# Where seven products and their weight sums stand among the up steps of an MLP

## The chip, the core and the metric

One core of a Trainium2 chip runs the whole program. The metric is device time in microseconds (us), lower is better. Of the engines, five names matter here: PE (TensorE, matmuls), DVE (VectorE), ACT (ScalarE), POOL (GpSimd, which here only issues DMAs) and SP (SyncE, which issues the other DMAs). Each engine runs its instructions in the order in which the compiled program lists them.

## The reference

Two residual layers of width D = 2048 over 256 tokens, in fp32: a convolution module, an MLP, a state-space layer, a second MLP, a final norm. The change touches the second MLP alone:

```python
def mlp(h, w_up, w_down):
    a = jax.nn.relu(h @ w_up)          # w_up 2048 x 8192
    return (a * a) @ w_down            # w_down 8192 x 2048
...
    h = rms_norm(x, mlp_norm[i])
    x = x + mlp(h, mlp_w_up[i], mlp_w_down[i])
return rms_norm(x, final_norm)
```

## The kernel before

**Precision.** Each fp32 weight block is split in two fp32r parts: ACT copies it to `hi` (L148) and DVE forms `lo = block - hi` (L155). Products are taken with both parts. A block is one *step* of the program, loaded, split and multiplied in two *halves* of 128 x 1024 elements (`run_steps`, L194). The four `hi` and four `lo` buffers let the split run up to four halves ahead of the products (L207); loads are issued four steps ahead (L205), and the six `raw` buffers hold three steps.

**The second MLP** works in eight slices s of 1024 hidden features.

- `up(s, k)`, written u0 to u7 below: eight steps that form slice s of `h @ w_up`. A half is 16 matmuls, eight with `hi` (L236, 512 columns) and eight with `lo` (L239, 256 columns). Every second one (odd k) ends with `relu2_forms` (L960), on ACT and DVE, which squares the activations and writes eight linear forms of them to `rT`.
- `seven(s, n)`, L753: the product with `w_down` for 1024 output columns, by a scheme of the Strassen-Winograd kind: seven products of 2 x 2 blocks where eight would be usual. They need sums of weight blocks. Its eight steps are called a0 to a7 for the first columns (n = 0) and b0 to b7 for the second (n = 2). A half of a product step is six matmuls of 512 columns (L743 to L745). The steps are:
  - a0: load block B01 into Y (POOL; no product).
  - a1: load B00, product A11; on DVE, X = B00 + Y, one add for each half.
  - a2: product S1 with X, nothing loaded.
  - a3: load B11, product S4; on DVE, X = B11 + X.
  - a4: product S2 with X, nothing loaded.
  - a5: a DMA of POOL adds B11 onto Y in place (L123), product S3 with Y.
  - a6: load B10, product A12.
  - a7: a DMA of POOL adds B10 onto X in place, product A22 with X.
  The sums of a1 and a3 are the adds at L161. Each product is taken into `x` by DVE (L772).

**Order.** A table in `mlp` (L905 to L909) lists the steps of round s: the eight up steps of slice s + 1 among the products of slice s. Rounds 0 to 5 have the same table; rounds 6 and the end have others. A scheduler at compile time then places instructions on each engine by readiness and priority; the split and the sums have a higher priority (`high_priority`, L147). `behind(ins)` (L451) holds it to one thing: what is issued inside comes after `ins`. Blocks for u, a1, a3 and a6 are loaded by SP in step order; those for a0, a5 and a7 by POOL.

Of the kernel before, what the change touches and what calls it, by code (L numbers as in the profile page):

```python
# [14 lines left out]
ALU = mybir.AluOpType  # L15
# [22 lines left out]
class Trunk:  # L38
# [97 lines left out]
    def split(self, h, urgent=True):  # L136
        i, half = divmod(h, 2)
        _, chain, consume, pre = self.steps[i]
        if consume is None:
            return None  # L140
        if pre == "x":
            sl = chain[half]
        else:
            sl = self.raws.pop(h)
        hi = self.w.tile(list(sl.shape), F32R, tag="hi", name="hi", bufs=4)
        lo = self.w.tile(list(sl.shape), F32R, tag="lo", name="lo", bufs=4)
        with self.tc.high_priority(offset=URGENT if urgent else 0):  # L147
            self.nc.scalar.activation(hi, sl, AF.Copy)  # L148
            eng = self.nc.gpsimd if i in self.pool_lo else self.nc.vector
            if self.barrier is not None and h == 2 * self.barrier + 2:  # L150
                self.low_late = lambda: eng.tensor_tensor(out=lo, in0=sl, in1=hi.bitcast(F32), op=ALU.subtract)
                self.parts[h] = (hi, lo)
                return None
            with self.behind(self.lo_gate) if self.lo_gate is not None else nullcontext():
                ins = eng.tensor_tensor(out=lo, in0=sl, in1=hi.bitcast(F32), op=ALU.subtract)  # L155
            self.lo_gate = None
            if i in self.also:
                to, first = self.also[i]
                if first is not None:
                    to[half] = self.wide.tile(list(sl.shape), F32, tag="wd", name="sum")  # L160
                self.tt(to[half], sl, (to if first is None else first)[half], ALU.add)  # L161
            if i in self.pool_lo:
                self.pool_ins = ins
            else:
                self.lo_ins = ins
        self.parts[h] = (hi, lo)
        return ins
# [566 lines left out]
    def mlp(self, layer, last_slice, last_block, hooks=None):  # L734
# [60 lines left out]
        def up(s, only=None):  # L795
            for q in range(4):
                for kc in range(2):
                    if only is not None and only != 2 * q + kc:
                        continue

                    def consume(hi, lo, half, q=q, kc=kc):
                        if kc == 0 and half == 0:
                            if formed(s):
                                if q % 2 == 0:
                                    rT.setdefault(s, []).append(self.blk_tile([P, 2, 2, 8, P], F32R, name="rT"))
                            elif q == 0:
                                rT[s] = self.blk_tile([P, 8, 2, T], F32R, name="rT")
                            rT["uacc"] = self.acc2()
                        A = rT["uacc"]
                        self.mm_f([A[:, 0], A[:, 1]], self.hT, hi, lo, kc * 8 + half * 4,  # L810
                                  kc == 0 and half == 0, kc == 1 and half == 1)
                        if kc == 1 and half == 1:
                            if s == 0 and q == 1 and layer == 0:
                                self.rate = 2.75
                            if formed(s):
                                act = lambda: self.relu2_forms(A, rT[s][q // 2][:, q % 2])
                            else:
                                act = lambda: self.relu2(A, rT[s], 2 * q)
                            act()
                    self.add_f(w_up, kc * 8, s * 1024 + q * 256, consume)  # L820
# [75 lines left out]
        m = [[seven(s, n) for n in (0, 2)] for s in range(nsl)]  # L896
        for k in range(7):
            up(0, k)
        m[0][0][0]()
        up(0, 7)  # L900
        for s in range(nsl - 1):
            u = [partial(up, s + 1, k) for k in range(8)]
            a, b = m[s]
            if s < nsl - 2:
                order = (u[0], a[1], a[2], u[1], a[3], a[4], u[2], a[5], a[6], u[3], b[0], a[7], b[1], u[4], b[2], b[6],  # L905
                         u[5], b[3], b[4], u[6], b[5], u[7], m[s + 1][0][0], b[7])
            else:
                order = (u[0], a[1], u[1], a[2], u[2], a[3], u[3], a[4], u[4], u[5], a[5], u[6], a[6], u[7],
                         m[s + 1][0][0], a[7])  # L909
            for e in order:  # L910
                e()
        a = m[-1][0]
# [854 lines left out]
```

## Time and profile before

| | |
|---|---|
| median of 3 runs | 1958.6 us (1958.26 to 1959.34) |
| profiled execution | 1959.17 us, span 1957.0 us |
| busy in the span | PE 99%, DVE 81%, ACT 55%, POOL 19% |
| rounds 0 to 5 of the second MLP | 1313.8 to 1819.6 us of the span |
| mean granted TensorE clock | 0.998 |

In a row of the timeline the first number is the start in us from the start of the span, the second the duration; an idle time before it and what ended that stand in brackets. Consecutive matmuls overlap in the records: the time that one takes of PE is the distance to the next one's start. The same holds on DVE, with a smaller overlap.

### The profile page before, as it was taken

To read this page: it belongs to the slowest core of one execution; us is meant where nothing else is said; L and a number is where in the kernel's file an instruction comes from. 1 tells how busy PE (TensorE), PEld (TensorE's weight loads), DVE (VectorE), ACT (ScalarE), POOL (GpSimd) and SP (SyncE) were. 2 spreads that over 40 slices of the span, in tenths; PEclk is the share of its full clock that TensorE was granted. 3 is DMA by queue.
4 is the path that set the end of the run, shared out by engine and by line. 5 is a ranking of instruction groups with operands and counts; after the bars stand their busy time and mean duration, and the time that the engine had idled before them with its cause. 6 is when DMAs were issued, how large, how long until landed. Compare 5 with 4: busy or idle time off the path is not lost.

```text
span 1957.0 us, 30302 instructions
## 1 busy us (share of the span) xinstructions
PE 1931.6 (99%) x11432; PEld 1653.2 (84%) x11432; DVE 1575.4 (81%) x2148; ACT 1083.5 (55%) x1357; POOL 363.2 (19%) x334
## 2 busy tenths in 40 slices
PE   8999999999999999999999999999999999999998
PEld 8999788888888888888888788888888888888887
DVE  6899898788787676767557856578999999999986
ACT  6444655544454545454545445466666666666664
POOL 4899300000010212221101000001111111111110
PEclk9999999999999999999999999999999999999999
DMA  9668468777686878877898966677889889898984
GB/s 249 183 178 222 127 193 258 216 232 235 208 268 183 210 215 262 270 246 230 279 328 304 352 210 186 191 226 216 245 248 255 258 239 256 234 253 242 254 262 137
DMA packets 334514, 457.96 MB, mean 234 GB/s; under 512 B 16481, under 2 KB 218273, under 8 KB 331009
## 3 DMA queue, kind: packets, MB, share of 16 engines
q1 hardware_dynamic: 299184, 369.93, 59.1%
q0 software_dynamic: 31616, 81.53, 17.6%
q10 hardware_dynamic: 3568, 4.56, 0.8%
q8 instruction: 89, 1.46, 0.3%
q14 instruction: 57, 0.47, 0.1%
HBM read 429.44 MB, written 34.91 MB: 237 GB/s over the span
## 4 chain that ended last, share of the span: by engine, by line
PE 89%; DVE 5%; DMA 3%; issue 2%; ACT 1%; POOL 0%; SPq 0%; DVEq 0%; POOLq 0%; ACTq 0%
PE acc L236 22%; PE acc L239 11%; PE acc L259 10%; PE acc L260 10%; PE acc L261 10%; PE acc L248 3%; PE acc L250 3%; PE acc L249 3%; DVE lo L155 3%; DMA raw<-in_mlp_w_down_dram 2%; PE mp L744 2%; PE mp L745 2%; PE mp L743 2%; PE mr L743 1%; PE mr L744 1%
## 5 line engine op out<-in xcount | busy, mean ns | idle before, releaser
L148 ACT ACTIVATE hi<-raw 128x1024 fp32r<-128x1024 f32 x644 | 681.3, 1059 | 743.1 <-PE acc L261 305.6
L155 DVE TENSOR_TENSOR lo<-raw,hi 128x1024 fp32r<-128x1024 f32 x583 | 708.1, 1221 | 275.7 <-ACT hi L148 274.4
L236 PE MATMUL acc<-hT,hi 128*128 128x512 f32 x2048 | 515.5, 393 | 0.0
L236 PEld LDWEIGHTS acc<-hT,hi 128*128 128x128 f32 x2048 | 372.4, 189 | 70.5 <-issue 1.6
L239 PEld LDWEIGHTS acc<-hT,lo 128*128 128x128 f32 x2048 | 279.3, 190 | 20.3 <-DVE lo L155 0.3
L239 PE MATMUL acc<-hT,lo 128*128 128x256 f32 x2048 | 286.1, 282 | 0.0
L259 PE MATMUL acc<-hi,rT 128*128 128x512 f32 x496 | 194.2, 392 | 0.0
L260 PE MATMUL acc<-lo,rT 128*128 128x512 f32 x496 | 193.4, 390 | 0.0
L261 PE MATMUL acc<-hi,rT 128*128 128x512 f32 x496 | 193.0, 389 | 0.0
L123 POOL DMA_DIRECT2D sum<-in_mlp_w_down_dram x56 | 68.1, 1231 | 462.5 <-DVE lo L155 301.0
L155 POOL TENSOR_TENSOR lo<-raw,hi 128x1024 fp32r<-128x1024 f32 x60 | 144.1, 2416 | 30.1 <-ACT hi L148 22.9
L248 PE MATMUL acc<-hT,hi 128*128 128x256 f32 x512 | 146.0, 286 | 1.0 <-ACT hi L148 1.0
L249 PE MATMUL acc<-hT,hi 128*128 128x256 f32 x512 | 145.2, 285 | 0.0
L250 PE MATMUL acc<-hT,lo 128*128 128x256 f32 x512 | 144.7, 285 | 0.1
L988 DVE SCALAR_TENSOR_TENSOR cv<-vT,dw,cv 128x256 f32<-128x256 f32 x348 | 140.9, 482 | 2.6 <-ACT cv L575 2.2
L148 ACT ACTIVATE hi<-sum 128x1024 fp32r<-128x1024 f32 x112 | 118.6, 1059 | 43.1 <-PE acc L236 26.2
L155 DVE TENSOR_TENSOR lo<-sum,hi 128x1024 fp32r<-128x1024 f32 x112 | 135.9, 1218 | 7.7 <-ACT hi L148 7.4
L259 PEld LDWEIGHTS acc<-hi,rT 128*128 128x128 f32 x496 | 93.1, 188 | 20.8 <-issue 1.6
L261 PEld LDWEIGHTS acc<-hi,rT 128*128 128x128 f32 x496 | 93.1, 188 | 19.4
L260 PEld LDWEIGHTS acc<-lo,rT 128*128 128x128 f32 x496 | 93.1, 188 | 19.0 <-issue 0.2
L248 PEld LDWEIGHTS acc<-hT,hi 128*128 128x128 f32 x512 | 98.5, 192 | 3.7 <-issue 2.1
L259 PE MATMUL acc<-hi,yT 128*128 128x512 f32 x256 | 101.1, 395 | 0.0
(324 smaller groups left out, 2957.9 us busy)
## 6 DMA issues: line engine op xcount, KB each, us to landing
raw<-in_mlp_w_up_dram SPq DMA_DIRECT2D x256, 512.0 KB, 4.8
raw<-in_mlp_w_down_dram SPq DMA_DIRECT2D x228, 512.0 KB, 5.5
sum<-in_mlp_w_down_dram POOLq DMA_DIRECT2D x84, 512.0 KB, 7.9
raw<-in_conv_w_in_dram SPq DMA_DIRECT2D x128, 256.0 KB, 3.9
raw<-in_ssm_w_glu_dram SPq DMA_DIRECT2D x64, 512.0 KB, 4.1
raw<-in_conv_w_out_dram SPq DMA_DIRECT2D x32, 512.0 KB, 4.2
Vd<-bv POOLq DMA_DIRECT2D x16, 512.0 KB, 5.3
Md<-Kd POOLq DMA_DIRECT2D x32, 256.0 KB, 6.9
```

The lines of the kernel that those rows point to most:

```text
L123: self.nc.gpsimd.dma_start(out=chain[hf], in_=view[:, k], accum_op=ALU.add)
L148: self.nc.scalar.activation(hi, sl, AF.Copy)
L155: ins = eng.tensor_tensor(out=lo, in0=sl, in1=hi.bitcast(F32), op=ALU.subtract)
L236: mm(accs[m], lhsT=hi[:, kk, cs[m]], rhs=xT(k0 + kk), start=first and kk == 0, stop=False)
L239: mm(accs[m][:, 0:T], lhsT=lo[:, kk, cs[m]], rhs=xT(k0 + kk)[:, 0, :], start=False, stop=last and kk == 3)
L248: mm(accs[m], lhsT=hi[:, kk, c], rhs=x[:, 0, :], start=first and kk == 0, stop=False)
L249: mm(accs[m], lhsT=hi[:, kk, c], rhs=x[:, 1, :], start=False, stop=False)
L250: mm(accs[m], lhsT=lo[:, kk, c], rhs=x[:, 0, :], start=False, stop=last and kk == 3)
L259: mm(acc[:, b, :], lhsT=ak[:, 0, t], rhs=hi[:, kk, :], start=first and kk == 0, stop=False)
L260: mm(acc[:, b, :], lhsT=ak[:, 0, t], rhs=lo[:, kk, :], start=False, stop=False)
L261: self.mm_last = mm(acc[:, b, :], lhsT=ak[:, 1, t], rhs=hi[:, kk, :], start=False, stop=last and kk == 1)
L988: return self.nc.vector.scalar_tensor_tensor(out=out, in0=a, scalar=s, in1=b, op0=op0, op1=op1)
```

## The change

Two things. In `split`, the add for X at L161 is issued `behind(ins)`, where `ins` is the subtraction that forms `lo` of the same half. And the tables of rounds 0 to 6 are written anew: the product steps stand one at a time or in twos between up steps, and b7 and a0 of the next slice move from the end of a round to behind the first up step of the next round (`late`).

```diff
                     to[half] = self.wide.tile(list(sl.shape), F32, tag="wd", name="sum")
-                self.tt(to[half], sl, (to if first is None else first)[half], ALU.add)
+                with self.behind(ins):
+                    self.tt(to[half], sl, (to if first is None else first)[half], ALU.add)
...
+        late = []
         for s in range(nsl - 1):
             u = [partial(up, s + 1, k) for k in range(8)]
             a, b = m[s]
             if s < nsl - 2:
-                order = (u[0], a[1], a[2], u[1], a[3], a[4], u[2], a[5], a[6], u[3], b[0], a[7], b[1], u[4], b[2], b[6],
-                         u[5], b[3], b[4], u[6], b[5], u[7], m[s + 1][0][0], b[7])
+                order = [u[0], *late, a[1], u[1], a[2], u[2], a[3], a[4], u[3], a[5], a[6], u[4], a[7], b[0], b[1],
+                         u[5], b[2], b[6], u[6], b[3], b[4], u[7], b[5]]
+                late = [b[7], m[s + 1][0][0]]
             else:
-                order = (u[0], a[1], u[1], a[2], u[2], a[3], u[3], a[4], u[4], u[5], a[5], u[6], a[6], u[7],
-                         m[s + 1][0][0], a[7])
+                order = [u[0], *late, a[1], u[1], a[2], u[2], a[3], u[3], a[4], u[4], u[5], a[5], u[6], a[6], u[7],
+                         m[s + 1][0][0], a[7]]
```

The instructions of the engines are the same in kind and number; their places differ. In the rows below the number behind a name tells buffers of one name apart; it differs between the two programs.

DVE in round 1, about step b3, before. `sum_13733` and `sum_13739` are X of the b steps, `raw_13830` and `raw_13832` the block of b3, `raw_13758` and `raw_13760` that of b6, `raw_13784` and `raw_13786` that of u5:

```order
L155 TENSOR_TENSOR lo_13811<-raw_13758,hi_13810 128x1024
L979 TENSOR_TENSOR sum_13733<-raw_13830,sum_13733 128x1024
L979 TENSOR_TENSOR sum_13739<-raw_13832,sum_13739 128x1024
L988 SCALAR_TENSOR_TENSOR v_13709<-v_13709,u_13708 128x128
L155 TENSOR_TENSOR lo_13835<-raw_13760,hi_13834 128x1024
L155 TENSOR_TENSOR lo_13846<-raw_13784,hi_13845 128x1024
L988 SCALAR_TENSOR_TENSOR x_83<-mr_13838,r2_12254,x_83 128x512
L155 TENSOR_TENSOR lo_13857<-raw_13786,hi_13856 128x1024
L274 TENSOR_TENSOR rT_13383<-v_13709,rT_13383 128x512
L155 TENSOR_TENSOR lo_13868<-raw_13830,hi_13867 128x1024
```

The same place after. `raw_13888` and `raw_13890` are the block of b3, `sum_13785` and `sum_13798` are X, `raw_13804` and `raw_13806` the block of b6, `raw_13830` and `raw_13832` that of u6:

```order
L155 TENSOR_TENSOR lo_13855<-raw_13804,hi_13854 128x1024
L155 TENSOR_TENSOR lo_13893<-raw_13806,hi_13892 128x1024
L970 TENSOR_TENSOR t_13874<-acc_13738,t_13874 128x512
L155 TENSOR_TENSOR lo_13904<-raw_13830,hi_13903 128x1024
L991 SCALAR_TENSOR_TENSOR x_83<-mr_13896,r2_12254,x_83 128x512
L155 TENSOR_TENSOR lo_13915<-raw_13832,hi_13914 128x1024
L155 TENSOR_TENSOR lo_13926<-raw_13888,hi_13925 128x1024
L982 TENSOR_TENSOR sum_13785<-raw_13888,sum_13785 128x1024
L982 TENSOR_TENSOR v_13876<-u_13875 128x2x128
L991 SCALAR_TENSOR_TENSOR x_83<-mq_13918,r2_12254,x_83 128x512
L155 TENSOR_TENSOR lo_13942<-raw_13890,hi_13941 128x1024
L982 TENSOR_TENSOR sum_13798<-raw_13890,sum_13798 128x1024
```

Before, both sums on b3's block stand ahead of the second `lo` of b6 and of both of u5, and eight rows ahead of the first `lo` of their own block. After, each stands right behind the `lo` of its own half, and every `lo` of the steps before b3 is ahead of it.

DVE in round 1, about steps a3 and a4, before. `rT_13026` is the second half of the forms of this round's slice (u6 and u7 of the round before), which S1 (a2) reads; `raw_13421` and `raw_13423` are the block of a3, `raw_13373` and `raw_13375` that of u1:

```order
L979 TENSOR_TENSOR sum_13364<-raw_13421,sum_13364 128x1024
L274 TENSOR_TENSOR rT_13026<-u_13325,rT_13026 128x512
L988 SCALAR_TENSOR_TENSOR v_13326<-v_13326,u_13325 128x128
L979 TENSOR_TENSOR sum_13381<-raw_13423,sum_13381 128x1024
L155 TENSOR_TENSOR lo_13437<-raw_13373,hi_13436 128x1024
L988 SCALAR_TENSOR_TENSOR v_13326<-v_13326,u_13325 128x128
L155 TENSOR_TENSOR lo_13448<-raw_13375,hi_13447 128x1024
L988 SCALAR_TENSOR_TENSOR x_83<-mp_13429,r2_12254,x_83 128x512
L155 TENSOR_TENSOR lo_13459<-raw_13421,hi_13458 128x1024
L155 TENSOR_TENSOR lo_13475<-raw_13423,hi_13474 128x1024
L274 TENSOR_TENSOR rT_13026<-v_13326,rT_13026 128x512
L155 TENSOR_TENSOR lo_13496<-sum_13364,hi_13495 128x1024
```

The same place after. `rT_12971` is that second half of the forms, `raw_13388` and `raw_13390` the block of u1, `sum_13402` and `sum_13415` X (whose `lo` is that of a2), `raw_13421` and `raw_13423` the block of u2, `raw_13447` the first half of that of a3:

```order
L155 TENSOR_TENSOR lo_13418<-raw_13388,hi_13417 128x1024
L991 SCALAR_TENSOR_TENSOR x_83<-mp_13046,r2_12254,x_83 128x512
L155 TENSOR_TENSOR lo_13426<-raw_13390,hi_13425 128x1024
L155 TENSOR_TENSOR lo_13437<-sum_13402,hi_13436 128x1024
L275 TENSOR_TENSOR rT_12971<-v_13309,rT_12971 128x512
L991 SCALAR_TENSOR_TENSOR x_83<-mp_13429,r2_12254,x_83 128x512
L155 TENSOR_TENSOR lo_13452<-sum_13415,hi_13451 128x1024
L155 TENSOR_TENSOR lo_13472<-raw_13421,hi_13471 128x1024
L155 TENSOR_TENSOR lo_13506<-raw_13423,hi_13505 128x1024
L970 TENSOR_TENSOR t_13491<-acc_13355,t_13491 128x512
L155 TENSOR_TENSOR lo_13517<-raw_13447,hi_13516 128x1024
L982 TENSOR_TENSOR sum_13402<-raw_13447,sum_13402 128x1024
```

Before, the last row of `relu2_forms` (`rT_13026<-v_13326`) stands behind the sums of a3, the four `lo` of u1 and a3 and behind both `lo` of a2, which are ahead of these rows; after, it stands between the two `lo` of a2, with u1 ahead of it and u2 and a3 behind it.

SP, the loads from the end of one round into the next; a row of `x2` is one block, since each half is one DMA:

```order
 L102 DMA raw<-in_mlp_w_up_dram 128x4x256 x2
 L102 DMA raw<-in_mlp_w_down_dram 128x2x512 x2
-L102 DMA raw<-in_mlp_w_up_dram 128x4x256 x6
+L102 DMA raw<-in_mlp_w_up_dram 128x4x256 x4
+L102 DMA raw<-in_mlp_w_down_dram 128x2x512 x2
+L102 DMA raw<-in_mlp_w_up_dram 128x4x256 x4
 L102 DMA raw<-in_mlp_w_down_dram 128x2x512 x2
 L102 DMA raw<-in_mlp_w_up_dram 128x4x256 x2
```

Where three blocks of `w_up` in a row (u6, u7 and u0 of the next round) came before, there are now at most two. POOL's DMAs stand in the same order as before.

## The prediction

> **What bounds the kernel now.** The page first:
>
> ```profile
> PE 1931.6 (99%) x11432; PEld 1653.2 (84%) x11432; DVE 1575.4 (81%) x2148; ACT 1083.5 (55%) x1357; POOL 363.2 (19%) x334
> ```
>
> PE is the bound, and the change takes no work from it. What can be won is time in which PE waits in rounds 0 to 5 of the second MLP, so the busy time by stage is read next, one stretch for each round (columns: stretch, length, then busy time of PE, PEld, DVE, ACT and POOL, granted clock, DMA share, GB/s):
>
> ```profile
> 1399.10:1481.80 82.70, 81.91 (x419) 69.35 (x418) 76.70 (x89) 55.39 (x63) 12.56 (x13) 1.00 0.91 250
> sum 505.80, PE 498.77 PEld 423.21 DVE 468.96 ACT 336.24 POOL 74.20; mean PE 83.13 PEld 70.53 DVE 78.16 ACT 56.04 POOL 12.37
> ```
>
> Three things lie close together: in 505.8 us PE's records leave 7.0 us open, DVE is busy 78.2 us of 84.3 in a mean round, and the DMA engines are about 0.9 busy. To know what PE loses, I need the price of its work where nothing waits, from PE's timeline:
>
> ```profile
> 1330.93 0.39 PE L744 MATMUL mr<-lo,rT 128*128 128x512 f32 x1
> ...
> 1335.69 0.39 PE L745 MATMUL mp<-hi,rT 128*128 128x512 f32 x1
> 1335.91 1.98 PE L236 MATMUL acc<-hT,hi 128*128 128x512 f32 x8
> 1337.73 1.12 PE L239 MATMUL acc<-hT,lo 128*128 128x256 f32 x8
> 1338.68 0.63 PE L236 MATMUL acc<-hT,hi 128*128 128x512 f32 x2
> ```
>
> Between 1330.93 and 1335.91 start 22 product matmuls: 0.2264 us each. A half of an up step takes 1338.68 - 1335.91 = 2.77 us. So an up step is 5.54 us, a product step (12 matmuls) 2.72 us, and a round (8 up steps, 14 product steps) 44.32 + 38.04 = 82.4 us. Six rounds are 494.2 us against 505.8: **PE loses 11.6 us**, 0.6% of the time, and no change of order can win more here. It is more than the 7.0 us of open time because a matmul that waited overlaps nothing, and because of one slow stretch, below. The waits of PE over these rounds (total, times, longest):
>
> ```profile
> PE mp L744 <- DVE lo L155: 3.1, 5, 0.6
> PE mq L744 <- DVE lo L155: 2.9, 3, 1.9
> PE mr L745 <- DVE rT L274: 1.0, 3, 0.6
> ```
>
> All end in DVE, and they are of two families. `mq` is product A12 (b6), `mp` and `mr` are those of a2 to a4.
>
> **Family B: a sum that waits for a DMA, with others behind it.** Timelines of DVE, PE and SP in round 0, and a stretch about it in the form of the table above:
>
> ```profile
> 1362.01 0.28 DVE L988 SCALAR_TENSOR_TENSOR v<-v,u 128x128 f32<-128x128 f32 x1
> 1366.17 1.23 DVE L979 TENSOR_TENSOR sum<-raw,sum 128x1024 f32<-128x1024 f32 x1 [3.88 <-DMA raw<-in_mlp_w_down_dram]
> 1367.31 1.22 DVE L155 TENSOR_TENSOR lo<-raw,hi 128x1024 fp32r<-128x1024 f32 x1
> 1368.45 1.22 DVE L979 TENSOR_TENSOR sum<-raw,sum 128x1024 f32<-128x1024 f32 x1
> ```
>
> ```profile
> 1366.28 0.39 PE L745 MATMUL mr<-hi,rT 128*128 128x512 f32 x1
> 1368.59 0.50 PE L744 MATMUL mq<-lo,rT 128*128 128x512 f32 x1 [1.93 <-DVE lo L155]
> 1370.30 3.36 PE L236 MATMUL acc<-hT,hi 128*128 128x512 f32 x8
> 1373.50 0.40 PE L744 MATMUL mq<-lo,rT 128*128 128x512 f32 x1
> ```
>
> ```profile
> 1356.46 2.16 SPq L102 DMA_DIRECT2D raw<-in_mlp_w_down_dram  x2
> ```
>
> ```profile
> 1360.00:1380.00 20.00, 18.07 (x87) 15.00 (x86) 15.84 (x18) 9.61 (x11) 1.10 (x1) 0.91 0.77 234
> ```
>
> SP issued b3's block at 1356.46 and it landed about 9.7 us later. DVE stood before b3's sum for 3.9 us, though the `lo` of b6 that PE needed at 1366.5 was next in its queue. PE started 2.08 us late (2.31 from start to start, less 0.23). Then eight L236 took 3.20 us instead of 1.82, another 1.4; with 0.3 about it the one event cost 3.8 us. The other two waits of `mq` (2.9 - 1.9 = 1.0 us) cost about 1.5 with the same 0.3 about each. Family B: 5.3 us.
>
> The slow stretch behind the wait shows in the granted clock: 0.91 in the last row, the 20 us about it. The Trainium skill, "TensorE: Matmul & The Clock Gate", Part 1 (the HAM clock gate), says that the clock halves after an idle window of about 3.4 us. By that rule a wait of 2.1 us would cost itself alone, and family B would be 1.4 us less; the row shows that it did cost them, so here rule and row differ.
>
> **Family A: too much of DVE's work in a row.** The five waits of `mp` in the list are one in each of rounds 1 to 5, among a2 to a4, some with one of `mr` ahead. Round 1, PE and DVE:
>
> ```profile
> 1416.84 0.39 PE L743 MATMUL mp<-hi,rT 128*128 128x512 f32 x1
> 1417.39 0.50 PE L745 MATMUL mr<-hi,rT 128*128 128x512 f32 x1 [0.16 <-DVE rT L274]
> 1418.53 0.50 PE L744 MATMUL mp<-lo,rT 128*128 128x512 f32 x1 [0.63 <-DVE lo L155]
> ```
>
> ```profile
> 1416.65 0.69 DVE L274 TENSOR_TENSOR rT<-v,rT 128x512 fp32r<-128x512 f32 x1
> 1417.26 1.22 DVE L155 TENSOR_TENSOR lo<-sum,hi 128x1024 fp32r<-128x1024 f32 x1
> 1418.39 0.68 DVE L967 TENSOR_TENSOR t<-acc,t 128x512 f32<-128x512 f32 x1
> 1418.99 0.74 DVE L988 SCALAR_TENSOR_TENSOR x<-mr,r,x 128x512 f32<-128x512 f32 x1
> 1419.65 1.22 DVE L155 TENSOR_TENSOR lo<-sum,hi 128x1024 fp32r<-128x1024 f32 x1
> 1420.78 0.42 DVE L979 TENSOR_TENSOR v<-u 128x256 f32<-128x256 f32 x1
> 1421.23 0.29 DVE L988 SCALAR_TENSOR_TENSOR v<-v,u 128x128 f32<-128x128 f32 x1
> 1421.44 1.22 DVE L155 TENSOR_TENSOR lo<-raw,hi 128x1024 fp32r<-128x1024 f32 x1
> ```
>
> Here DVE runs back to back and PE waits for it twice: 0.33 us (0.55 less 0.22 from 1416.84) and 0.91 (1.14 less 0.23). Family A is what is left of the loss: 11.6 - 5.3 = 6.3 us, 1.3 for each of five rounds.
>
> **The change, part by part.** DVE's prices are distances of starts in those rows: `lo` 1.13 us, a sum 1.14 (1367.31 to 1368.45 for the `lo` ahead of it, the same shape), a take into `x` 0.66, and `relu2_forms` 0.60 + 0.45 + 2 x 0.21 + 2 x 0.61 = 2.7. Against PE's prices a step gives DVE this much room: u with even k 5.54 - 2.26 = +3.3; u with odd k +0.6; a product without sums 2.72 - 2.26 - 0.66 = -0.2; one with sums (a1, a3, b1, b3) -2.5.
>
> *The table.* Before, u0 is followed by a1, a2, u1, a3, a4: -2.5 - 0.2 + 0.6 - 2.5 - 0.2 = -4.8 before u2 gives room again. That is family A. The other stretches of that table (a5, a6, u3, a7, b1; b2, b6, u5, b3, b4) come to -2.5, and there PE waits only when a DMA is late. After, the worst stretches (a3, a4, u3, a5, a6; a7, b1, u5, b2, b6) come to -2.5, the two others to -2.3. So what cost 1.3 us a round becomes what cost nothing. The last row of `relu2_forms` for u7, for which `mr` waited, also gains: u1 now lies between a1 and a2, 5.5 us more. **Family A: -6.3 us.** What covers a stretch of -2.5 is the split's lead of four halves; if it is lost, 2.5 us a round come back.
>
> *The sum behind `lo`.* The head of DVE's queue is no longer a sum on a block still under way: the `lo` of b6 and u6 are ahead of it. The block itself has more time: its first buffer comes free with the first `lo` of u5, and from there to b3's first `lo` the compiled order has 7 `lo`, 3 takes, one rT and one t, 11.1 us, where 7.1 us of work (4 `lo`, 2 takes, three rows of `relu2_forms`) stood between u4's first `lo` and the sum. The landing took 9.7 us here and 7.2 in the median (below). **Family B: -5.3 us.** If the block is late still, DVE waits at b3's `lo`, with all of b6 and u6 done: PE has those 8 us to go on.
>
> *b7 and a0 behind u0.* Nothing is added. a0's load into Y may start when b5's `lo` has read the old Y, and a1's sum needs it: 9 us of DVE's work lie between now. b7's block may be added onto X after b4's `lo`; 10.6 us of DVE's work lie between that and b7's `lo` (11.2 before). Counted the same way. From the DMA views of the six rounds:
>
> ```profile
> sum<-in_mlp_w_down_dram POOLq DMA_DIRECT2D x71, 512.0 KB, 7.9
> raw<-in_mlp_w_down_dram SPq DMA_DIRECT2D x70, 512.0 KB, 7.2
> DMA to landing us min/median/max: 6.0/8.0/11.1
> ```
>
> (The last row is that of the adding DMAs, L123.) With 1.2 us to issue and 1.1 for ACT's `hi`, 8.0 makes 10.3: just in time; 11.1 makes 13.4: 2.8 late. Bounds: 0, and 2.8 us in each of six rounds, 17 us, if none of it is covered. I take the value near the median landing, **+2.5 us** in all: one wait of 0.4 us a round, like the smaller ones in the rows above.
>
> *Round 6 and the end* have other tables; round 6 gets b7 behind its u0 as the others do, and shows no wait of its own before: 0.
>
> Sum: 1959.17 (this execution: 1957.0 of span and 2.2 around it) - 6.3 - 5.3 + 2.5 = 1950.1; the median of the runs shown is 0.6 below this execution, so **1949.5 us**, -0.46%.
>
> **The rivals.**
>
> *1. The late adds.* b7, a0 and a1 now bring three blocks (3 MB) close together, at a DMA share of 0.9. If L123 lands at its worst, DVE waits up to 2.8 us at b7 with a1's `lo` and sums behind. PE's cover there: a1's first half can be split once u0's first half is done, 5.5 us ahead of need, of which 1.1 + 1.1 go into the split and 1.1 + 0.8 into rows behind it: some 1.5 us are free. So 1.3 to 2.8 us a round, 8 to 17 in all: 1955 to 1964, most of it within 0.2% of before. For it: the share of 0.9 and the 11.1. Against: a7, b0 and b1 stood together the same way before. The Trainium skill, "DMA: Bandwidth & Descriptors", section "Issuing engines are not separate DMA queues", has all queues run on the same 16 DMA engines, so POOL's adds would be slowed by SP's loads; the trace agrees as far as w_down's loads go: 7.2 us in these rounds, 5.5 in the whole span (sixth part of the page).
>
> ```profile
> raw<-in_mlp_w_down_dram SPq DMA_DIRECT2D x228, 512.0 KB, 5.5
> ```
>
> *2. Slower: sums that no longer fill.* Before, a sum can run while ACT still makes `hi` of its block; behind `lo` it can't. If DVE then stands for ACT's 1.06 us at each of the eight sums of a round, that is 8.5 us of idle, 4.3 more than the 4.2 that DVE has free (82.4 - 78.2), 26 us in six rounds: 1958.6 - 11.6 + 26 = 1973. It turns to a loss of time from 6.1 us of idle a round. Rows of round 1 (idle ahead, and for whom):
>
> ```profile
> L155 DVE TENSOR_TENSOR lo<-raw,hi 128x1024 fp32r<-128x1024 f32 x27 | 32.5, 1215 | 1.3 <-ACT hi L148 1.3
> L155 DVE TENSOR_TENSOR lo<-sum,hi 128x1024 fp32r<-128x1024 f32 x16 | 19.4, 1216 | 0.8 <-ACT hi L148 0.8
> ```
>
> DVE stood 2.1 us a round for `hi` over 43 `lo`: it is mostly behind ACT, which speaks against this.
>
> *3. No effect.* The waits are not a matter of order, but of DVE's 95% load, and move to other steps: 1956 to 1960.
>
> **How the numbers follow.** The forecast gets 0.70; rival 1 gets 0.17 (0.14 within 0.2%, 0.03 slower), rival 2 gets 0.09, rival 3 gets 0.04. What a measurement here can tell from no change is about 0.2%, 3.9 us. So faster 0.70, same 0.18, slower 0.12. Low end: all 11.6 won, 1947.0, and 0.4 for scatter: 1946.6. High end: the forecast and most of rival 1, leaving out its upper part and rival 2: 1959.0.
>
> **What would show it.** Right: round lengths of 82.4 to 83 us; no wait of PE for rT among a2 to a4; no DVE sum that waits for a DMA of `raw`; no stretch with a clock under 1. Rival 1: waits of ACT or DVE for `sum<-in_mlp_w_down_dram` at b7 or a1, and PE waiting at a1. Rival 2: DVE's idle ahead of `lo<-raw` for ACT well over 2.1 us a round. I am wrong if the rounds stay at 84 us with other names in the list of PE's waits.

## The result and the profile after

| | before | after |
|---|---|---|
| median | 1958.97 us (4 runs, 1958.26 to 1962.48) | 1947.88 us (4 runs, 1947.77 to 1948.21) |
| ratio to before, 95% interval | | 0.9938 [0.9926, 0.9951] |
| profiled execution: time, span | 1959.17, 1957.0 us | 1947.79, 1946.0 us |
| PE's start-to-start loss in rounds 0 to 5 | 11.7 us | 0.7 us |

All medians and ratios here and below are of fast executions alone; two of the ten of two_passes_in_u6, 2732 and 6819 us, were slow ones.

The last row of the table is what the whole case turns on. It is read from PE's timeline: the distance from each matmul's start to the next one's, less the usual distance of that shape (0.2275 us for 512 columns, 0.120 for 256), summed where more than 0.04 us is left. It comes to 11.7 us for before, where the prediction had 11.6 from the prices of the steps.

The page after, parts 1 and 4 (busy time; the chain of work that ended last, as shares of the span by engine):

```profile
PE 1927.5 (99%) x11432; PEld 1652.8 (85%) x11432; DVE 1575.1 (81%) x2148; ACT 1081.4 (56%) x1357; POOL 363.2 (19%) x334
PE 96%; DVE 2%; DMA 1%; issue 0%; SPq 0%; ACT 0%; POOL 0%; POOLq 0%; DVEq 0%; ACTq 0%
```

DVE's busy time has not changed by a microsecond; PE's is 4.1 us less. The chain has changed: before, PE held 89% of it, DVE 5%, DMA 3%. What went from the span is, for the most part, time in which PE stood.

The table by stage, in the form of the prediction's (stretch, length, busy time of PE, PEld, DVE, ACT and POOL, granted clock, DMA share, GB/s), for four of rounds 1 to 5, each from u0's start to the next u0's start:

```profile
1391.25:1474.44 83.19, 83.08 (x427) 70.80 (x425) 79.06 (x91) 56.06 (x65) 12.73 (x13) 1.00 0.90 250
1474.44:1557.30 82.86, 82.86 (x427) 70.79 (x425) 79.06 (x91) 56.06 (x65) 12.71 (x13) 1.00 0.92 257
1557.30:1640.18 82.88, 82.88 (x426) 70.78 (x425) 79.05 (x91) 56.05 (x65) 12.68 (x13) 1.00 0.91 254
...
1723.04:1805.90 82.86, 82.86 (x426) 70.79 (x425) 79.07 (x91) 56.07 (x65) 12.71 (x13) 1.00 0.90 254
```

PE's records leave 0.1 us open in round 1 (83.2 us) and nothing in the others (82.9 us), and the clock is 1.00 throughout. The work of all six rounds now runs from 1313.93 to 1805.90 and, since the last b7 has moved behind that point, 2.72 us more: 494.7 us against 505.8, 11.1 less. The span is 11.0 shorter. Everything was won here.

PE's list of waits over the second MLP is empty. The largest of DVE's over rounds 0 to 5, before and then after (engine and line, released by: total, times, longest):

```profile
DVE sum L979 <- DMA raw<-in_mlp_w_down_dram: 17.6, 13, 3.9
DVE lo L155 <- ACT hi L148: 15.8, 19, 2.1
```

```profile
DVE lo L155 <- ACT hi L148: 22.0, 34, 1.3
DVE x L991 <- PE mp L746: 1.8, 6, 0.3
```

Seventeen microseconds of waiting for a block still under way are gone, and only 6 more stand ahead of `lo`, where DVE waits for ACT. ACT in turn waits mostly for PE to give a `hi` buffer back (its two longest rows):

```profile
ACT hi L148 <- PE acc L237: 80.3, 64, 2.0
ACT hi L148 <- PE mp L746: 32.5, 36, 1.4
```

That is the harmless kind of idle time: DVE stands there because it is as far ahead as the buffers allow.

The place of family B after, DVE in round 1 about the sums of b3:

```profile
1457.10 2.35 DVE L155 TENSOR_TENSOR lo<-raw,hi 128x1024 fp32r<-128x1024 f32 x2
1459.37 1.22 DVE L982 TENSOR_TENSOR sum<-raw,sum 128x1024 f32<-128x1024 f32 x1
1460.50 0.42 DVE L982 TENSOR_TENSOR v<-u 128x256 f32<-128x256 f32 x1
1460.84 0.74 DVE L991 SCALAR_TENSOR_TENSOR x<-mq,r,x 128x512 f32<-128x512 f32 x1
1461.50 1.21 DVE L155 TENSOR_TENSOR lo<-raw,hi 128x1024 fp32r<-128x1024 f32 x1
1462.63 1.21 DVE L982 TENSOR_TENSOR sum<-raw,sum 128x1024 f32<-128x1024 f32 x1
1463.77 0.68 DVE L275 TENSOR_TENSOR rT<-u,rT 128x512 fp32r<-128x512 f32 x1
1464.37 0.28 DVE L991 SCALAR_TENSOR_TENSOR v<-v,u 128x128 f32<-128x128 f32 x1
1464.57 1.22 DVE L155 TENSOR_TENSOR lo<-sum,hi 128x1024 fp32r<-128x1024 f32 x1
```

Both sums run without a bracket, so without idle time ahead. The last row is the first `lo` of b4; it ends at 1465.79, and this is where PE needs it:

```profile
1466.16 0.39 PE L746 MATMUL mr<-hi,rT 128*128 128x512 f32 x1
1466.38 0.39 PE L745 MATMUL mp<-lo,rT 128*128 128x512 f32 x1
```

DVE is 1466.38 - 1465.79 = 0.6 us ahead of PE. I call this distance the **lead** of a `lo`: from its end on DVE to the start of the first matmul that reads it. It is the smallest of the round; the next is 1.4 us, at a4 (1.1 in rounds 2 to 5). Most lie between 2 and 5. In the table below, a lead of 0.1 or 0.2 means that PE stood waiting for that `lo`.

### The profile page after: what moved, and what is told of

Same layout as the page of the kernel before. It is cut to its first block, busy times and chain, and to the rows that moved or that the text cites. A ratio compares the mean times of both kernels' runs of the same rounds, so it can differ in the third digit from the quotient of the medians.

```text
span 1946.0 us, 30310 instructions
## 1 busy us (share of the span) xinstructions
PE 1927.5 (99%) x11432; PEld 1652.8 (85%) x11432; DVE 1575.1 (81%) x2148; ACT 1081.4 (56%) x1357; POOL 363.2 (19%) x334
## 4 chain that ended last, share of the span: by engine, by line
PE 96%; DVE 2%; DMA 1%; issue 0%; SPq 0%; ACT 0%; POOL 0%; POOLq 0%; DVEq 0%; ACTq 0%
PE acc L237 24%; PE acc L240 12%; PE acc L260 10%; PE acc L261 10%; PE acc L262 10%; PE acc L251 3%; PE acc L249 3%; PE acc L250 3%; PE mp L745 3%; PE mp L744 3%; PE mp L746 3%; PE mr L744 1%; PE mr L745 1%; PE mr L746 1%; PE acc L270 1%; PE acc L271 1%
```

## The experiments

Each kernel is timed beside runs of the kernel before on the same chip, which had medians of 1959.5 to 1960.1 us there; the ratio is to those runs. "Loss" is PE's start-to-start loss in rounds 0 to 5. A lead is the smaller one of the step's two halves, in round 1.

| kernel | median us | ratio [95%] | loss us | lead at a4, b6, b4 |
|---|---|---|---|---|
| before | 1958.97 | | 11.7 | 0.1, 0.2, 0.4 |
| sum_behind_old_table | 1957.36 | 0.9987 [0.9979, 0.9996] | 10.3 | 0.1, 2.6, 1.1 |
| table_alone | 1959.51 | 0.9995 [0.9987, 1.0004] | 10.7 | 2.2, 0.6, 2.0 |
| table_late_sums_of_a3_b3 | 1947.75 | 0.9941 [0.9929, 0.9954] | 0.0 | 2.1, 2.7, 0.6 |
| after | 1947.88 | 0.9938 [0.9926, 0.9951] | 0.7 | 1.4, 2.7, 0.6 |
| old_table_two_takes_out | 1948.01 | 0.9941 [0.9929, 0.9953] | 0.8 | 1.4, 3.1, 1.1 |
| spread_without_late | 1956.81 | 0.9986 [0.9977, 0.9995] | 9.0 | 1.1, 2.7, 0.6 |
| b5_beside_b4_b7_late | 1955.41 | 0.9983 [0.9973, 0.9992] | 7.7 | 1.5, 2.7, 0.2 |
| two_passes_in_u3 | 1954.65 | 0.9972 [0.9961, 0.9984] | 7.5 | 1.1, 2.0, 0.6 |
| two_passes_in_a6 | 1953.81 | 0.9970 [0.9960, 0.9980] | 5.6 | 1.4, 3.3, 0.1 |
| two_passes_in_u6 | 1958.95 | 0.9998 [0.9988, 1.0007] | 11.6 | 1.1, 2.7, 0.1 |
| two_passes_spread | 1953.12 | 0.9962 [0.9949, 0.9974] | 5.5 | 0.1, 2.5, 0.1 |
| two_passes_u7_u0 | 1955.65 | 0.9981 [0.9972, 0.9990] | 8.0 | 1.8, 2.5, 0.6 |
| six_passes_even | 1969.36 | 1.0048 [1.0034, 1.0061] | 20.3 | |

### Each half of the change alone

sum_behind_old_table is the kernel before with the first part of the change's diff alone:

```diff
-                self.tt(to[half], sl, (to if first is None else first)[half], ALU.add)
+                with self.behind(ins):
+                    self.tt(to[half], sl, (to if first is None else first)[half], ALU.add)
```

table_alone is the changed kernel with these lines taken back.

> The table of before, with each sum behind the lo of its half. My terms: family B (a sum that waits for a block, with b6 behind it) goes, 5.3 us; family A (DVE's stretch a1 to a4) stays, 6.3 us. So about 1959.0 - 5.3 = 1953.7 us, PE waiting among a2 to a4 in rounds 1 to 5 and no longer at b6. Rival, the sums' place is all of it (family A came from sums that held up the forms and the lo of a4): 1948. Rival, the table is all of it: 1959.

> The new table, with the sums placed freely as before. My terms: family A goes, 6.3 us; b3's sum still stands ahead of a lo of b6 and of u6 with its block only 6.5 us of DVE's work behind the release of its buffer, so DVE still waits for the DMA and PE loses up to 5.3 us at b6: about 1952.7 us. Rival, the table alone gives DVE lead enough to hide these waits: 1948 us, DVE's waits for raw in the list but no wait of PE.

Both missed, by 3.7 and 6.8 us. PE's list of waits in the second MLP, for sum_behind_old_table:

```profile
PE mp L745 <- DVE lo L155: 6.6, 4, 1.7
PE mr L744 <- DVE x L989: 1.2, 1, 1.2
PE mr L745 <- DVE lo L155: 0.5, 1, 0.5
```

and for table_alone:

```profile
PE acc L239 <- DVE lo L155: 6.6, 6, 1.4
PE acc L269 <- DVE lo L155: 1.7, 1, 1.7
PE mq L744 <- DVE lo L155: 1.4, 2, 0.9
```

In the first, all is lost among a2 to a4, 1.9 us in each of rounds 1 to 5 (2.5 in round 2), and nothing at b6: family B is gone, and family A has grown from 6.3 to 10.3 us. In the second there is nothing at a2 to a4, and 0.7 to 3.0 us a round, nearly all at b6 and the up step behind it: family A is gone, and family B has grown from 5.3 to 10.7 (2.0 more, the row of L269, lie behind round 6). DVE of table_alone in round 1 shows that B is the same mechanism as before:

```profile
1456.69 1.23 DVE L981 TENSOR_TENSOR sum<-raw,sum 128x1024 f32<-128x1024 f32 x1 [2.94 <-DMA raw<-in_mlp_w_down_dram]
1457.83 1.22 DVE L155 TENSOR_TENSOR lo<-raw,hi 128x1024 fp32r<-128x1024 f32 x1
```

So each edit removes the waits that the prediction gave to it, and neither is seen to win more than 0.13% alone. Only both together win 0.62%.

### Which sums it is

table_late_sums_of_a3_b3 is the changed kernel with only the sums of a3 and b3 held behind `lo`, those of a1 and b1 left free:

```diff
-                with self.behind(ins):
+                with self.behind(ins) if first is None else nullcontext():
```

> The new table, with only the sums of a3 and b3 (X = block + X) behind their lo; those of a1 and b1 stay free. Family B as I put it comes from b3's sum alone: 1948 to 1949 us, no wait of PE at b6 or u6. Rival, all sums count alike: halfway between table_alone and the changed kernel, 1953.

It loses nothing at all, and takes 1947.75 us, as fast as the change within 0.13 us. So holding back the sums of a3 and b3 is enough to remove family B; those of a1 and b1 play no part in it. The waits of table_alone lie at b6 and u6, beside b3, but a3's sums and b3's were not tried apart.

### Whether family A is DVE's stretch of work

old_table_two_takes_out is sum_behind_old_table without two of the takes into `x` of the stretch:

```diff
-                                if c is not None:
+                                if c is not None and not (n0 == 0 and form in (A11, S1) and s < nsl - 2):
```

> As sum_behind_old_table, but without the takes of a1 and a2 into x in rounds 0 to 5 (their part of the output is left out): 1.3 us less of DVE's work within a1 to a4. That kernel lost 10.3 us, nearly all of it at the lo of a4 (1.9 us a round). If the stretch of DVE's work decides, the loss falls by about 1.3 us in each of rounds 1 to 5: 1957.4 - 6.5 = 1951 us. If the chain a3's lo, sum, hi and lo of a4 decides, whatever else stands there: 1957.

It took 1948.01 us, 3 us less than expected, and the loss goes from 10.3 to 0.8 us. The way from a3's first sum to a4's first `lo` is as long as before, 4.0 us from start to start in both traces, so it was not this chain that took too long. But the run doesn't show that the amount of work decides either. It takes out 1.3 us of DVE's work a round, and PE gains 1.9 us in each of the five rounds and a lead of 1.3 to 1.4 us at a4 besides: some 3 us in all. The record shows a second cause that fits. One of the two takes is that of S1 (a2) out of the bank `mr`, and S4 (a3) is added onto this bank, so PE may begin a3 only when the take is done. PE and DVE of sum_behind_old_table in round 1:

```profile
1413.03 0.40 PE L744 MATMUL mp<-hi,rT 128*128 128x512 f32 x1
1415.08 0.50 PE L745 MATMUL mp<-lo,rT 128*128 128x512 f32 x1 [1.66 <-DVE lo L155]
1416.58 0.39 PE L744 MATMUL mr<-hi,rT 128*128 128x512 f32 x1
```

```profile
1413.81 1.22 DVE L155 TENSOR_TENSOR lo<-sum,hi 128x1024 fp32r<-128x1024 f32 x1
1414.95 0.74 DVE L989 SCALAR_TENSOR_TENSOR x<-mr,r,x 128x512 f32<-128x512 f32 x1
```

While PE stands, all twelve matmuls of a3 (2.7 us) are still ahead of it, in the order that the compiler gave, with a3's two `lo` formed 6.9 and 5.4 us before PE reads them; the take that a3 needs ends at 1415.69. In the kernel before it is the same: a3's `lo` are 4.6 and 4.9 us early, PE waits for a4's, and begins a3 at 1420.00, behind the take that starts at 1418.99. Without S1's take, in old_table_two_takes_out, PE begins a3 right behind a2, and all that is left is 0.8 us at a2 in round 1. So family A is shown to be DVE's lateness among a2 to a4; whether the amount of its work or this one take decides was not separated. The new table helps against both, since u2 now lies between a2 and a3.

### The other places in the table

spread_without_late has the new table with b7 and a0 at the end of the round, and b5 ahead of u7; b5_beside_b4_b7_late moves only b7 back behind the next u0:

```diff
-                         u[5], b[2], b[6], u[6], b[3], b[4], u[7], b[5]]
-                late = [b[7], m[s + 1][0][0]]
+                         u[5], b[2], b[6], u[6], b[3], b[4], b[5], u[7], m[s + 1][0][0], b[7]]
```

```diff
-                         u[5], b[2], b[6], u[6], b[3], b[4], b[5], u[7], m[s + 1][0][0], b[7]]
+                         u[5], b[2], b[6], u[6], b[3], b[4], b[5], u[7], m[s + 1][0][0]]
+                late = [b[7]]
```

> The changed kernel, but b7 and a0 of the next slice stay at the end of the round, and b5 moves beside b4: u6, b3, b4, b5, u7, a0, b7, then u0, a1. The stretch b3, b4, b5 comes to -2.9 us, with u7 and b7 behind it; Y has as much time as before. If moving b7 and a0 behind u0 is a detail: 1948 to 1950 us. Rival, it carries part of the gain because two more products in a row pass the cover: PE waits at b4, b5 or b7 in every round, 1 us each, 1954 us or more.

> spread_without_late with b7 alone behind u0 of the next round: b3, b4, b5, u7, a0, then u0, b7, a1. There ACT waited 20 us for the DMA that adds b7's block onto X, which may start when b4 is split: between b4 and b7 stood b5 and u7, 8.3 us of PE, now also u0, 13.8 us as in the changed kernel. If that DMA is the cause of the 9 us: 1948 to 1949 us, no wait of ACT for sum<-in_mlp_w_down_dram. If it is b4 and b5 side by side, or a0's place: 1955 to 1957.

In spread_without_late, ACT waits for the adding DMA, which its expectation did not name:

```profile
ACT hi L148 <- DMA sum<-in_mlp_w_down_dram: 20.0, 9, 3.2
```

In b5_beside_b4_b7_late this wait is gone from the list, and yet the loss only goes from 9.0 to 7.7 us. So the DMA of b7 was not the main cause. All 7.7 us lie at u7, in each round, and so do 7.4 of the 9.0 us of the other kernel. PE and DVE of b5_beside_b4_b7_late at u7 and b5:

```profile
1471.06 2.11 PE L237 MATMUL acc<-hT,hi 128*128 128x512 f32 x8 [0.15 <-ACT hi L148]
1474.04 1.22 PE L240 MATMUL acc<-hT,lo 128*128 128x256 f32 x8 [0.87 <-DVE lo L155]
1476.93 0.39 PE L744 MATMUL mp<-hi,rT 128*128 128x512 f32 x1
```

```profile
1469.89 2.36 DVE L155 TENSOR_TENSOR lo<-sum,hi 128x1024 fp32r<-128x1024 f32 x2
1472.76 1.22 DVE L155 TENSOR_TENSOR lo<-raw,hi 128x1024 fp32r<-128x1024 f32 x1
```

Though the table has b5 ahead of u7, the compiler let PE begin u7 (1471.06) before b5 (1476.93), while DVE forms both `lo` of b5 first. These have leads of 6.1 and 6.3 us; u7's first `lo` behind them has 0.1, against 1.8 in the changed kernel. So b5's place is what costs here, by an order on DVE that is not PE's, and no wait was found that comes from a0's.

### How much more DVE can take, and where

These kernels are the changed one with `lo` formed a second time in some halves of rounds 0 to 5; the values do not change. Each second pass is 1.13 us of DVE's work.

```diff
+            if h in self.twice:
+                with self.behind(ins):
+                    ins = eng.tensor_tensor(out=lo, in0=sl, in1=hi.bitcast(F32), op=ALU.subtract)
...
+                    if layer == 1 and 0 < s < nsl - 1:
+                        self.twice |= {2 * len(self.steps) + hf for k, hf in ((3, 0), (3, 1)) if k == 2 * q + kc}
```

The list of (k, half) is that of u3 here; `(2, 0), (6, 0)` in two_passes_spread, both halves of u6 in two_passes_in_u6, both of u0, u2 and u4 in six_passes_even, `(7, 1), (0, 1)` in two_passes_u7_u0. For two_passes_in_a6 the same is set where step a6 is issued.

> The changed kernel with both lo of u3 formed twice in rounds 0 to 5: two more passes of DVE, 2.3 us a round, in the stretch a3, a4, u3, a5, a6, whose balance falls from -2.5 to -4.8 us, that of a1 to a4 before. DVE has 78.2 + 2.3 = 80.5 us of work in a round of 82.8 us. If the stretch decides, PE loses what it lost at a2 to a4 before, about 1.3 us a round: 1947.9 + 8 = 1956 us, waits at a5 or a6. If only DVE's total in a round decides, nothing is lost: 1948. If the old waits came from the late forms (rT) alone, nothing is lost either, since rT of this round is long written: 1948.

> The same two more passes a round, one in the first half of u2 and one in that of u6, both up steps with 3.3 us of room. No stretch gets worse than -2.7 us. If the stretch decides: 1948 us, less than 1.5 us lost. If the total decides at a DVE share of 97%, the same loss as with both passes in u3.

> The changed kernel with both lo of u0, u2 and u4 formed twice in rounds 0 to 5: six more passes, 6.8 us of DVE a round. DVE then has 78.2 + 6.8 = 85.0 us of work in a round that PE does in 82.8. If DVE's total becomes the bound: at least 6 x 2.2 = 13 us more than the changed kernel, 1961 us, DVE without idle. If every pass costs as in the two runs with two passes (0.4 to 0.5 us of 1.13 a pass): 6 x 6 x 0.45 = 16 us, 1964. If the passes lie in room that nothing else uses: 1950 or less.

> The changed kernel with both lo of a6 formed twice in rounds 0 to 5, 2.3 us more of DVE a round. New theory (two steps ahead): with four buffers DVE splits a step while PE runs the step two places before it, so what counts is DVE's work on step k against PE's time for step k - 2. a6 is split while PE runs u3, 5.54 us long, with 2.26 of split and 0.66 of a take: 2.6 us are free and take the two passes. 1948 to 1949 us, no wait of PE. By my old account (DVE's work and PE's time of the same step): a3, a4, u3, a5, a6 falls to -4.8 us, as with both passes in u3, which cost 6.8 us: 1955.

> Both lo of u6 formed twice instead. Two steps ahead: u6 is split while PE runs b2 (2.72 us), beside the forms of u5 (2.7 us) and ahead of b3 with its sums, split while PE runs b6 (2.72 us): that stretch falls from -4.7 to -7.0 us. One pass there cost 0.7 us a round in two_passes_spread, the second costs another 1.1: 1.8 us a round, 1947.9 + 11 = 1959 us, waits at b3 or b4. By my old account u6 has 3.3 us of room, and 1.0 is left: 1948, at most 0.5 us a round, 1951.

The same 2.26 us a round cost 0.9 to 1.9 us a round (5.5 to 11.6 us in six), by where they stand, and none of these four kernels is free of loss. In two_passes_in_u3 PE waits at the second pass itself, not at a5 or a6, so that is in part an effect of where the compiler put the pass. In two_passes_in_a6, half a round ahead of b4, PE nevertheless waits at b4:

```profile
1469.22 0.50 PE L748 MATMUL mp<-lo,rT 128*128 128x512 f32 x1 [0.77 <-DVE lo L155]
```

Leads of 2.4 and 2.6 us at the doubled step come down to 1.4 and 1.6, and between a6 and b4 they do not come all the way back, though u4 and u6 lie between, each of which leaves DVE 3.3 us by the account of room per step. For u6, two steps ahead of b4, the lead table gives 2.26 - 0.6 = 1.7 us a round; 1.9 was measured. The expectation for two_passes_in_u6 was met and that for two_passes_in_a6 was not: "two steps ahead" falls, and so does the account of room that starts afresh at each up step. In two_passes_spread, too, the second passes stand in up steps with even k, which had room by that account, and PE waits at a4 and b4 instead. six_passes_even misses the other way, at 1969.36 us slower than expected: three times the work of the other kernels loses 20.3 us, against 5.5 to 11.6. There DVE's total is all but the bound: it is busy 85.6 us in a mean round of 86.5 us (1426.28 to 1599.24, two rounds). The expectation reckoned from 78.2 us of work a round; the changed kernel has 79.1 in each of rounds 1 to 5, and 6.8 more is 85.9, 3.0 more than the 82.9 that PE needs.

The last kernel puts the two passes where the leads are largest (3.4 us at the second half of u7, 5.8 at that of u0) and DVE stands idle right behind.

> The changed kernel with lo of the second half of u7 and of the second half of u0 formed twice in rounds 0 to 5: twelve more subtractions, 12 x 1.13 = 13.6 us of DVE's work, as much as in two_passes_in_u3, two_passes_in_a6 and two_passes_in_u6. Theory 'lead': what counts is how far DVE's lo is ahead of PE's use of it at that place and at all places behind it until DVE next stands idle for want of a free hi or lo buffer. In the changed kernel's trace the lead is only 0.6 us at b4 and 1.4 us at a4, but 3.4 us at the second half of u7 and 5.8 us at that of u0, and DVE then stands 1.1 and 0.3 us idle at b7 and 1.3 us at a2, so that these 2.3 us a round are used up before a4 is reached. It expects no PE wait: 1948.0 to 1949.0 us, start-to-start loss under 1 us. Rival 'load': DVE at some 98% of a round can't be fed any more work, wherever it stands, and the waits come out at the thinnest place: 1953.5 to 1959, as in the three runs named.

It took 1955.65 us, inside the range of the rival. But PE waits for no `lo`: the leads are no shorter than the lead theory had them, 0.6 at b4 and 1.8 at a4, and PE's whole list is this.

```profile
PE mr L747 <- DVE x L996: 5.5, 5, 1.1
```

It waits for the take of S1 again, ahead of a3. DVE of the changed kernel at that place, then of this one:

```profile
1414.40 1.23 DVE L155 TENSOR_TENSOR lo<-raw,hi 128x1024 fp32r<-128x1024 f32 x1 [1.29 <-ACT hi L148]
1415.54 1.22 DVE L982 TENSOR_TENSOR sum<-raw,sum 128x1024 f32<-128x1024 f32 x1
1416.68 0.74 DVE L991 SCALAR_TENSOR_TENSOR x<-mr,r,x 128x512 f32<-128x512 f32 x1
```

```profile
1417.54 1.22 DVE L987 TENSOR_TENSOR sum<-raw,sum 128x1024 f32<-128x1024 f32 x1
1418.68 1.22 DVE L155 TENSOR_TENSOR lo<-raw,hi 128x1024 fp32r<-128x1024 f32 x1
1419.81 1.22 DVE L987 TENSOR_TENSOR sum<-raw,sum 128x1024 f32<-128x1024 f32 x1
1420.95 0.42 DVE L987 TENSOR_TENSOR v<-u 128x256 f32<-128x256 f32 x1
1421.29 0.68 DVE L278 TENSOR_TENSOR rT<-u,rT 128x512 fp32r<-128x512 f32 x1
1421.89 0.74 DVE L996 SCALAR_TENSOR_TENSOR x<-mr,r,x 128x512 f32<-128x512 f32 x1
```

With the two passes in, the compiler placed the take of S1 behind a3's second `lo`, both sums and two rows of `relu2_forms`; before them, it stood behind the first sum. It now starts at 1421.89, and PE's first matmul of S4 at 1422.68; this costs 1.6 us in each of rounds 1 to 5. So the run does not tell the theories apart by its time. It shows that lead has to be counted for everything of DVE's that PE waits for, the takes of S1 as well as each `lo`, and that an insertion also moves what stands far behind it. Whether the two passes would be free with the take in its old place was not tried.

## Why the prediction was right, point by point

1. **PE loses 11.6 us in rounds 0 to 5, and no more can be won.** Right: the trace's own starts give 11.7, and 11.0 of them were won.
2. **Two families of waits, and both go.** Right for the two edits together. Family B has the cause that the prediction named: sums waiting for their block held up the `lo` behind them (table_alone and table_late_sums_of_a3_b3). For family A the prediction named too much of DVE's work in a row. That DVE is late there is shown, but not that the amount is why: the prediction did not see that all of a3 stood behind the wait with its `lo` ready, held by the take of S1, and old_table_two_takes_out takes out that take together with the work.
3. **Family A: -6.3 us by the table. Family B: -5.3 us by the sums.** The sum held, but as two separate terms they did not: alone, the table leaves 10.7 us of B and the sums leave 10.3 of A. A price of a wait is read from a trace in which the other wait also stands, and PE standing at one place is time in which DVE gets ahead for the next. The terms could be added here only because both were removed. Why A grows from 1.3 to 1.9 us a round when B goes was not taken apart further.
4. **b7 and a0 behind u0: "nothing is added", +2.5 us given back.** This is the term that was mis-sized: 2.5 us less the 0.7 that PE still loses makes 1.8, about the 1.6 us between forecast and result. The adding DMA did not land sooner than before, rather later in the median:

```profile
DMA to landing us min/median/max: 6.0/8.4/10.8
```

   (before: 6.0, 8.0 and 11.1). Yet neither ACT nor DVE waits for `sum<-in_mlp_w_down_dram` in their lists. The count of 10.6 us of work against 10.3 agrees with that, and what I took for it, 0.4 us a round, was a guess near the median that no run shows. That the place matters a little is shown by spread_without_late, where ACT waits 20.0 us for that DMA and PE loses 1.3 us more than with b7 late.
5. **The account of room per step.** It ranked the stretch of before (-4.8) above those of after (-2.5), which was right. It did not find the tightest place after: b4, with 0.6 us of lead, in a stretch of -2.3. The step that failed is that room in an up step makes good what was lost before it. two_passes_in_a6 shows that DVE carries a loss of lead over u4 and u6 to b4.
6. **Rival 1, the late adds:** did not come about (point 4). **Rival 2, sums that no longer fill:** DVE does stand more for `hi`, 22.0 us in six rounds against 15.8, 3.7 a round, but the prediction's limit of 6.1 us a round is far, and none of it fell where PE needed something. **Rival 3, waits that move to other steps:** not in the change as a whole; but each of its halves alone ends one family of waits, and the other grows by 4.0 to 5.4 us.
7. **What was to be seen:** rounds of 82.9 us (round 1: 83.2, a little over the 83 named), no wait for rT among a2 to a4, no sum waiting for a block, no clock under 1. All four are in the rows above.

## What to carry to other kernels

When two groups of waits in a stage hang on one engine, removing one of them may be worth nothing, as here: what one place gained was lost at the other. Judge a change of order by the smallest lead in the whole cycle (end of the producer's instruction to the start of its first reader), for every result that the bound engine waits for, and not by the waits that are now listed nor by the balance of single steps. In an engine that runs in order, put nothing that depends on a late transfer ahead of work that is ready and wanted sooner; a sum placed behind the `lo` of its own block cost nothing here, where that `lo` needs the same block anyway. And before an experiment that takes work out of an engine is read as a matter of amount, look whether another engine waits for that very work.

## What was not expected of the hardware

The clock. In the kernel before, a distance of 2.31 us between the starts of two matmuls was followed by the 0.91 of the prediction's row, a mean over 20 us. A narrower stretch of the same trace, in the same columns:

```profile
1369.80:1373.20 3.40, 3.40 (x9) 2.66 (x9) 3.40 (x5) 1.58 (x2) 0.00 (x0) 0.50 0.75 194
```

So for 3.4 us the granted clock was half, from 1.2 us behind the end of the wait; it was 1.00 from 1366.0 to 1369.8 and from 1373.2 to 1380.0. In table_alone PE stood nearly as long,

```profile
1896.74 0.39 PE L744 MATMUL mr<-lo,rT 128*128 128x512 f32 x1
1898.87 0.50 PE L269 MATMUL acc<-lo,rT 128*128 128x512 f32 x1 [1.74 <-DVE lo L155]
1899.21 0.40 PE L270 MATMUL acc<-hi,rT 128*128 128x512 f32 x1
```

2.13 us from start to start, and the matmuls behind it follow at 0.24 us, with a granted clock of 1.00 from 1890 to 1930. Four waits of sum_behind_old_table, with 2.05 or 2.06 us from start to start in rounds 1, 3, 4 and 5, were followed by 1.00 as well. Only one event in these traces was followed by a slow clock, so no threshold follows; a wait of about 2 us may or may not cost more than itself here.
